# Gate and up of five feed-forward layers made transposed, with the weights held still

## The chip, the core and the metric

The kernel runs on one core of one Trainium2 chip. The metric is the device time in microseconds of one execution, the median over runs. Engines are named as the profile names them: PE is the matrix engine (PEld its weight loads), DVE the vector engine, ACT the scalar engine, POOL the general one, SP the one that issues most transfers.

## The reference, cut

256 tokens of width 1024 pass five gated feed-forward layers (hidden width 2816) with a mixer of attention or convolution between them. One layer of the first block, and the form that the other four have:

```python
def rms_norm(x, g):
    y = x * lax.rsqrt(jnp.mean(x * x, axis=-1, keepdims=True) + EPS)
    return y * g

h = rms_norm(x, norm2_g)                                   # first block
x = x + (silu(h @ w_gate) * (h @ w_up)) @ w_down

def swiglu(h, wg, wu, wd):                                 # second block, four times
    return (silu(h @ wg) * (h @ wu)) @ wd
h = rmsnorm(x, g[0])
x = x + 0.5 * rmsnorm(swiglu(h, wg, wu, wd), g[1])
```

## The kernel before

Tokens are two tiles of 128 rows, t = 0 and 1, whose residual stays in `xres`. Every matrix product is done in three parts for accuracy: each operand is split into a high part (float32r, rounded) and a low part (the rest), and high·high, high·low and low·high are added up in PSUM (`mm3`, lines 270 to 272).

Weights come as blocks of 1 MB (128 partitions by 2048 columns) in the fixed order of `PLAN`. `load` brings a block into one of three `raw` buffers on SP's queue; `split` makes of it two pairs of tiles `wh` and `wl`, one ACT copy (line 240) and one DVE subtraction (line 241) of 1024 columns for each. There are 8 buffers of each kind, so four blocks. `take` hands out the next block and issues the splits ahead of it.

The input of a layer is `xT`, the residual transposed, multiplied by the gain and split: a tile of the high part and a tile of the low part, each with 8 pieces of 128 columns for both t (`norm_in`, lines 306 to 312). The factor 1/rms of a token (`rstd`, one value for each row) isn't in it; it is applied to the results.

In `ffn` the pieces of `xT` (128 by 128) are the stationary operand and 512 columns of weights the moving one. So a bank `mm` gets 128 tokens by 512 hidden columns, for gate and for up, t = 0 and 1: four banks for a chunk of 512 columns, five chunks, and a last one of 256. ACT takes the SiLU of gate times `rstd` (line 455) and DVE multiplies it by up times `rstd` (line 456). The product has the tokens on its rows, and the down projection needs the hidden columns there, so `transposes` turns each tile with 128 by 128 transposes on PE (line 414), and ACT and DVE split what comes out (lines 416 and 417). Transposes of a chunk stand behind the gate of the next chunk, those of the last chunk in the down projection.

The down projection takes 11 blocks into four banks. `ends` then calls `finish` (sum of squares, power -0.5 on POOL, a product with the gain `post`, an addition to `xres`, lines 369 to 382) and `norm_in` of the next layer. The first feed-forward has no `post` and adds its banks to `xres` directly (line 361).

A scheduler sets the order on each engine from priorities; the order that is quoted below is what it made.

Of the kernel before, what the change touches and what calls it, by code (L numbers as in the profile page):

```python
# [53 lines left out]

FF_FULL = 5
FF_LAST = 2560


def ffn_blocks(g, u, d, idx):
    out = []
    for c in range(FF_FULL):
        out += proj_blocks(g, idx, c * 512, 512) + proj_blocks(u, idx, c * 512, 512)
    out += proj_blocks((g, u), idx, FF_LAST, 512)
    for k in range(0, 22, 2):
        out.append((d, idx, k, 2, 0, 1024))
    return out
# [107 lines left out]
class K:  # L176
# [121 lines left out]
    def norm_in(self, t, idx):  # L298

        nc = self.nc  # L300
        xh, xl = self.x_halves(t)
        for b in range(2):
            tp = self.tpt()
            for j in range(4):
                k = b * 4 + j
                nc.tensor.transpose(tp[:, j * P : (j + 1) * P], self.xres[t][:, k * P : (k + 1) * P], self.ident)  # L306
            for j in range(4):
                k = b * 4 + j
                c = slice(k * P, (k + 1) * P)
                g = self.cols[:, C_G + idx * 8 + k : C_G + idx * 8 + k + 1]  # L310
                nc.scalar.activation(xh[:, c], tp[:, j * P : (j + 1) * P], AF.Copy, scale=g)  # L311
                nc.vector.scalar_tensor_tensor(  # L312
                    xl[:, c], tp[:, j * P : (j + 1) * P], g, xh[:, c].bitcast(F32), op0=ALU.mult, op1=ALU.subtract)

    def x_halves(self, t):

        if t == 0:
            self.xT = [self.xp.tile([P, 2 * D], F32R, tag=n, name=self.nm(n)) for n in ("xh", "xl")]
        return [a[:, t * D : (t + 1) * D] for a in self.xT]

    def start(self):

        nc = self.nc
        nc.scalar.dma_start(self.cols[:, C_G : C_G + 8], self.cols_in[:, C_G : C_G + 8])
        self.x_halves(0)
        xh, xl = [a[:, :].rearrange("p (t c) -> p t c", t=2) for a in self.xT]
        parts = []
        for p in range(4):
            r = (self.raw if p < 3 else self.gp).tile(
                [P, 2048], F32, tag="raw" if p < 3 else "bias", name=self.nm("first"))  # L330
            for a, n in ((0, 768), (768, 768)) if p < 2 else ((0, 1536),):
                nc.sync.dma_start(r[:, a : a + n], self.first_in[p][:, a : a + n])
            wh = self.hl.tile([P, 1024], F32R, tag="wh", name=self.nm("wh"))
            wl = self.hl.tile([P, 1024], F32R, tag="wl", name=self.nm("wl"))
            for j in range(2):
                k = 2 * p + j
                c, o = slice(k * P, (k + 1) * P), slice(j * 512, (j + 1) * 512)
                g = self.cols[:, C_G + k : C_G + k + 1]
                x = r[:, j * 768 : j * 768 + 256].rearrange("p (t c) -> p t c", t=2)
                u = r[:, j * 768 + 256 : (j + 1) * 768]  # L340
                nc.scalar.activation(wh[:, o], u, AF.Copy)
                nc.scalar.activation(xh[:, :, c], x, AF.Copy, scale=g)  # L342
                nc.vector.tensor_tensor(wl[:, o], u, wh[:, o].bitcast(F32), op=ALU.subtract)
                nc.vector.scalar_tensor_tensor(  # L344
                    xl[:, :, c], x, g, xh[:, :, c].bitcast(F32), op0=ALU.mult, op1=ALU.subtract)
            parts.append((wh, wl))
        self.blk += [[None, parts[:2]], [None, parts[2:]]]
        self.nload = self.nsplit = 2

    def xlhs(self, t):  # L350
        xh, xl = [a[:, t * D : (t + 1) * D] for a in self.xT]
        return lambda k: (xh[:, k * P : (k + 1) * P], xl[:, k * P : (k + 1) * P])

    def finish(self, t, ps, post, half_scale):

        nc = self.nc
        x = self.xres[t]
        if post is None:
            for h in range(2):
                c = slice(h * 512, (h + 1) * 512)  # L360
                nc.vector.tensor_tensor(x[:, c], x[:, c], ps[h], op=ALU.add)
# [40 lines left out]
    def ffn(self, post_row, half_scale, nxt):  # L402
        nc = self.nc
        post = self.row_bcast(post_row, D) if post_row is not None else None
        hT = {}
        pend = None

        def transposes(p):
            c, cw, hs = p
# [11 lines left out]
        for c in range(FF_FULL + 1):  # L421
            cw, nb = (512, 2) if c < FF_FULL else (256, 2)
            pg = [None, None]
            pu = [None, None]
            if c == 0:
                gb = self.take(nb, 2)
                pg[0], pu[0] = self.mmt(cw), self.mmt(cw)
                for i, b in enumerate(gb):
                    self.block_mm(pg[0], b, self.xlhs(0), 0, i == 0, i == nb - 1)
                ub = self.take(nb, 0)  # L430
                for i, b in enumerate(ub):
                    self.block_mm(pu[0], b, self.xlhs(0), 0, i == 0, i == nb - 1)
                pg[1], pu[1] = self.mmt(cw), self.mmt(cw)
                for ps, bs in ((pg[1], gb), (pu[1], ub)):
                    for i, b in enumerate(bs):
                        self.block_mm(ps, b, self.xlhs(1), 0, i == 0, i == nb - 1)
            elif c == FF_FULL:
                both = self.project()
                for t in range(2):
                    pg[t], pu[t] = both[t][:, :cw], both[t][:, cw:]  # L440
                transposes(pend)
            else:
                for pp in (pg, pu):
                    pp[0], pp[1] = self.mmt(cw), self.mmt(cw)
                    for i in range(nb):
                        (b,) = self.take(1)
                        for t in range(2):
                            self.block_mm(pp[t], b, self.xlhs(t), 0, i == 0, i == nb - 1)
                    if pp is pg and pend is not None:
                        transposes(pend)  # L450
            hs = []
            for t in range(2):
                r = self.rstd[t][:, 0:1]
                sg = self.slot()
                nc.scalar.activation(sg[:, :cw], pg[t], AF.Silu, scale=r)  # L455
                nc.vector.scalar_tensor_tensor(sg[:, :cw], pu[t], r, sg[:, :cw], op0=ALU.mult, op1=ALU.mult)  # L456
                hs.append(sg)
            pend = (c, cw, hs)
        ps = [[self.mmt(), self.mmt()] for _ in range(2)]

        def down(t, b, first, last):
# [5 lines left out]
        for i in range(9):  # L467
            (b,) = self.take(1)
            for t in range(2):
                down(t, b, i == 0, False)  # L470
            if i == 0:
                transposes(pend)
# [7 lines left out]
        self.ends(ps, post, half_scale, nxt)  # L480

    def ends(self, ps, post, half_scale, nxt):
        nc = self.nc
        for t in range(2):
            with self.tc.high_priority(offset=HP):
                self.finish(t, ps[t], post, half_scale)
                if nxt is not None:
                    self.norm_in(t, nxt)
                else:
# [690 lines left out]
```

## Time and profile before

| | us |
|---|---|
| median of 3 runs | 1333.37 (1333.33 to 1336.2) |
| the profiled execution | 1331.7 |
| its span, first to last instruction | 1329.5 |
| mean granted PE clock, share of full speed | 0.995 |
| PE busy | 1301.0 (98%) |
| DVE, ACT, POOL busy | 766.3 (58%), 679.9 (51%), 41.0 (3%) |

The time is that of the span and 2.2 us around it. Matmuls are pipelined: a PE row has the time from a matmul's start to its modelled end, and the next one starts before that end. The pace is read from the starts of rows that follow each other, not from the duration of one.

### The profile page before, as it was taken

Reading aid. Unit: us, or ns where it says so; the run is one execution under the profiler, and the core shown is the slowest. Engines: PE = TensorE matmul, PEld = TensorE weight load, DVE = VectorE, ACT = ScalarE, POOL = GpSimd, SP = SyncE. Lnnn points to the kernel's source line nnn. Section 1 sums busy time; section 2 is a strip of 40 time slices with the busy share of each in tenths; the row PEclk is TensorE's granted clock in tenths of the full one; section 3 lists DMA queues with packets and bytes.
Section 4 is the critical chain, followed back from the end, with each engine's and each line's share of the span. In section 5 each row is a group of like instructions: output and inputs, shape, how many; then the busy total and the mean of one; then the engine's idle time right before and its main releaser. Section 6 shows DMA issues by size and latency. Waiting matters only on the chain.

```text
span 1329.5 us, 16379 instructions
## 1 busy us (share of the span) xinstructions
PE 1301.0 (98%) x6382; PEld 1057.5 (80%) x6382; DVE 766.3 (58%) x1167; ACT 679.9 (51%) x1067; POOL 41.0 (3%) x59
## 2 busy tenths in 40 slices
PE   9789999999999999999999999999999999999997
PEld 7567788888888888777888888888888777888886
DVE  6654655545655548896755555655546555755543
ACT  6455554445545436746644444644435855754431
POOL 0310000000000000000000000000000000000000
PEclk9899999999999999999999999999999999999999
DMA  9943555554555545442465554655454453455540
GB/s 353 285 146 116 190 190 188 191 176 173 192 190 188 189 164 192 143 154 99 152 226 180 189 187 159 237 179 187 172 192 172 162 187 113 177 202 190 190 158 32
DMA packets 37502, 238.10 MB, mean 179 GB/s; under 512 B 4272, under 2 KB 7088, under 8 KB 10416
## 3 DMA queue, kind: packets, MB, share of 16 engines
q1 hardware_dynamic: 36064, 234.31, 50.2%
q0 software_dynamic: 640, 2.16, 0.7%
q8 instruction: 50, 0.82, 0.2%
q10 hardware_dynamic: 720, 0.59, 0.1%
q14 instruction: 28, 0.23, 0.0%
HBM read 235.40 MB, written 1.64 MB: 178 GB/s over the span
## 4 chain that ended last, share of the span: by engine, by line
PE 89%; DVE 3%; ACT 2%; DMA 1%; issue 1%; POOL 0%; ACTq 0%; DVEq 0%; POOLq 0%; SPq 0%
PE mm L272 27%; PE mm L270 27%; PE mm L271 27%; PE tp L414 2%; PE at L621 1%; PE mm L812 1%; PE tp L575 1%; PE tp L306 1%; DVE wl L241 1%; DMA cw<-cw 1%; PE at L690 1%; PE tp L648 1%; PE at L966 0%; ACT e L628 0%; ACT wh L240 0%
## 5 line engine op out<-in xcount | busy, mean ns | idle before, releaser
L241 DVE TENSOR_TENSOR wl<-raw,wh 128x1024 fp32r<-128x1024 f32 (+1 forms) x422 | 508.8, 1219 | 422.4 <-ACT wh L240 409.6
L240 ACT ACTIVATE wh<-raw 128x1024 fp32r<-128x1024 f32 (+1 forms) x422 | 439.5, 1056 | 511.3 <-PE mm L272 474.4
L270 PE MATMUL mm<-wh,xh 128*128 128x512 f32 (+1 forms) x1168 | 459.5, 393 | 1.4 <-ACT xh L342 0.9
L272 PE MATMUL mm<-wh,xl 128*128 128x512 f32 (+1 forms) x1168 | 456.9, 392 | 0.1
L271 PE MATMUL mm<-wl,xh 128*128 128x512 f32 (+1 forms) x1168 | 455.8, 390 | 0.0
L270 PEld LDWEIGHTS mm<-wh,xh 128*128 128x128 f32 x1168 | 220.0, 188 | 47.6 <-ACT xh L311 1.7
L272 PEld LDWEIGHTS mm<-wh,xl 128*128 128x128 f32 x1168 | 219.7, 188 | 46.3 <-DVE xl L344 0.8
L271 PEld LDWEIGHTS mm<-wl,xh 128*128 128x128 f32 x1168 | 220.0, 188 | 44.7 <-issue 0.7
L270 PE MATMUL mm<-wh,slot 128*128 128x512 f32 x536 | 210.5, 393 | 1.3 <-ACT slot L564 1.3
L272 PE MATMUL mm<-wh,slot 128*128 128x512 f32 x536 | 209.5, 391 | 0.6 <-DVE slot L565 0.6
L271 PE MATMUL mm<-wl,slot 128*128 128x512 f32 x536 | 209.5, 391 | 0.0
L270 PEld LDWEIGHTS mm<-wh,slot 128*128 128x128 f32 x536 | 100.7, 188 | 23.3 <-issue 1.7
L272 PEld LDWEIGHTS mm<-wh,slot 128*128 128x128 f32 x536 | 100.7, 188 | 21.8 <-DVE slot L565 1.0
L271 PEld LDWEIGHTS mm<-wl,slot 128*128 128x128 f32 x536 | 100.7, 188 | 19.9
L456 DVE SCALAR_TENSOR_TENSOR slot<-mm,rstd,slot 128x512 f32<-128x512 f32 (+1 forms) x60 | 41.8, 703 | 18.2 <-PE mm L272 18.2
L311 ACT ACTIVATE xh<-tp,cols 128x128 fp32r<-128x128 f32 x112 | 37.3, 370 | 24.8 <-PE tp L306 14.4
L312 DVE SCALAR_TENSOR_TENSOR xl<-tp,cols,xh 128x128 fp32r<-128x128 f32 x112 | 35.6, 347 | 15.4 <-ACT xh L311 14.1
L628 ACT ACTIVATE e<-e,mx 128x128 f32<-128x128 f32 (+1 forms) x80 | 35.3, 445 | 6.9 <-DVE mx L625 6.9
L455 ACT ACTIVATE slot<-mm,rstd 128x512 f32<-128x512 f32 (+1 forms) x60 | 36.4, 657 | 3.5 <-PE mm L272 3.4
L417 DVE TENSOR_TENSOR slot<-tp,slot 128x512 fp32r<-128x512 f32 (+1 forms) x60 | 35.9, 639 | 0.0
L369 ACT ACTIVATE junk<-mm 128x512 bf16<-128x512 f32 x24 | 14.4, 601 | 36.3 <-PE mm L272 36.3
L283 POOL TENSOR_TENSOR pr<-pm,mhalf 128x1 f32<-128x1 f32 x12 | 6.6, 550 | 855.8 <-DVE pm L373 855.8
(122 smaller groups left out, 642.1 us busy)
## 6 DMA issues: line engine op xcount, KB each, us to landing
raw<-w SPq DMA_DIRECT2D x209, 1024.0 KB, 4.9
gb<-rows SPq DMA_DIRECT2D x7, 512.0 KB, 5.5
cw<-cw SPq DMA_DIRECT2D x2, 1024.0 KB, 14.0
bias<-rev SPq DMA_DIRECT2D x2, 1024.0 KB, 5.7
xc<-h POOLq DMA_DIRECT2D x4, 394.5 KB, 13.6
first<-first SPq DMA_DIRECT2D x4, 384.0 KB, 4.5
first<-first SPq DMA_DIRECT2D x2, 768.0 KB, 7.8
raw<-w SPq DMA_DIRECT2D x2, 592.0 KB, 3.7
```

Of the source, the lines that this page charges most:

```text
L240: self.nc.scalar.activation(wh[:, o], r[:, i_], AF.Copy)
L241: self.nc.vector.tensor_tensor(wl[:, o], r[:, i_], wh[:, o].bitcast(F32), op=ALU.subtract)
L270: mm(ps, xh, wh, start=start, stop=False)
L271: mm(ps, xh, wl, start=False, stop=False)
L272: mm(ps, xl, wh, start=False, stop=stop)
L311: nc.scalar.activation(xh[:, c], tp[:, j * P : (j + 1) * P], AF.Copy, scale=g)
L312: nc.vector.scalar_tensor_tensor(xl[:, c], tp[:, j * P : (j + 1) * P], g, xh[:, c].bitcast(F32), op0=ALU.mult, op1=ALU.subtract)
L414: nc.tensor.transpose(tp[:, j * P : (j + 1) * P], hs[t][:, j * P : (j + 1) * P], self.ident)
L417: nc.vector.tensor_tensor(hlo[:, :cw], tp, hh[:, :cw].bitcast(F32), op=ALU.subtract)
L455: nc.scalar.activation(sg[:, :cw], pg[t], AF.Silu, scale=r)
L456: nc.vector.scalar_tensor_tensor(sg[:, :cw], pu[t], r, sg[:, :cw], op0=ALU.mult, op1=ALU.mult)
L628: nc.scalar.activation(s[:, :nk], s[:, :nk], AF.Exp, bias=mx[:, h : h + 1], scale=-1.0, accum_out=sm[:, h : h + 1])
```

## The change

The first 512 columns of gate and up stay as they were. The other 2304 are made in nine pairs of 256 gate and 256 up columns. Now 128 columns of weights are the stationary operand, and the moving one is x: `xT` becomes one tile in which, for each of the 8 pieces, the high part of all 256 tokens and the low part stand side by side (512 columns). `wh` against all 512 columns gives high·high in the left half of a bank and high·low in the right half; `wl` against the left 256 columns adds low·high to the left half. A bank so holds 128 hidden columns by 256 tokens twice, and the two halves are added when it is emptied (an ACT copy, a DVE addition). The result has the hidden columns on its rows, as the down projection needs them; it isn't transposed.

`rstd` now differs along the columns. For gate it is made into a tile `R` by two transposes for each layer (`rstd_rows`) and multiplied in by DVE before the SiLU. For up it is left out: it is one factor of each token, so `finish` applies it to the result of down. The blocks are as many and as large as before.

```diff
+        def cols_T():
+            (b,) = self.take(1)
+            z = self.slot()
+            for f in range(2):
+                bank = self.mmt()
+                for k in range(8):
+                    self.mm3_T(bank, k, *self.part(b, k * 256 + f * P, P), k == 0, k == 7)
+                zf = z[:, f * 256 : (f + 1) * 256]
+                nc.scalar.activation(zf, bank[:, :256], AF.Copy)
+                nc.vector.tensor_tensor(zf, zf, bank[:, 256:], op=ALU.add)
+            return z
+
+        for c in range(FF_PAIRS):
+            g = cols_T()
             if c == 0:
...
+                R = self.rstd_rows()
+            v2 = lambda z: z[:, :].rearrange("p (f n) -> p f n", f=2)
+            nc.vector.tensor_tensor(v2(g), v2(g), R[:, :256].unsqueeze(1).broadcast_to([P, 2, 256]), op=ALU.mult)
+            nc.scalar.activation(g, g, AF.Silu)
+            if c == 0:
+                transposes(pend)
+            u = cols_T()
+            nc.vector.tensor_tensor(g, u, g, op=ALU.mult)
+            hh, hlo = self.slot(F32R), self.slot(F32R)
+            nc.scalar.activation(hh, g, AF.Copy)
+            nc.vector.tensor_tensor(hlo, g, hh[:, :].bitcast(F32), op=ALU.subtract)
+            for f in range(2):
                 for t in range(2):
...
+    def mm3_T(self, bank, k, wh, wl, start, stop):
+
+        x = self.xT[:, k * 512 : (k + 1) * 512]
+        mm = self.nc.tensor.matmul
+        mm(bank, wh, x, start=start, stop=False)
+        mm(bank[:, :256], wl, x[:, :256], start=False, stop=stop)
...
+    def rstd_rows(self):
+
+        nc = self.nc
+        rb, R = self.slot(), self.slot()
+        for t in range(2):
+            nc.vector.tensor_copy(rb[:, t * P : (t + 1) * P], self.rstd[t][:, 0:1].broadcast_to([P, P]))
+        nc.scalar.activation(R[:, :256], self.transpose4(rb, 2), AF.Copy)
+        return R
...
+        if row is not None:
+            r2 = self.small(1, "pr2")
+            nc.vector.tensor_scalar(r2, row, row[:, 0:1], c0, op0=ALU.mult, op1=ALU.mult)
+            c0 = r2[:, 0:1]
...
-                nc.vector.tensor_tensor(y, ps[h], post[:, h * 512 : (h + 1) * 512], op=ALU.mult)
+            pc = post[:, h * 512 : (h + 1) * 512]
+            if row is None:
+                nc.vector.tensor_tensor(y, ps[h], pc, op=ALU.mult)
+            else:
+                nc.vector.scalar_tensor_tensor(y, ps[h], row[:, 0:1], pc, op0=ALU.mult, op1=ALU.mult)
```

On PE, in the first feed-forward of the kernel before, the gate and up of a chunk and the eight transposes behind them stand so (`xh` and `xl` are the two tiles of `xT`):

```order
L270 MATMUL mm_1433<-wh_1448,xh_1233 128x512
L271 MATMUL mm_1433<-wl_1449,xh_1233 128x512
L272 MATMUL mm_1433<-wh_1448,xl_1234 128x512
L414 MATMUL tp_1520<-sh,slot_1426 128x128 x4
L414 MATMUL tp_1529<-sh,slot_1429 128x128 x4
L270 MATMUL mm_1538<-wh_1454,xh_1233 128x512
```

The changed kernel has at that place, where the gate of the first pair ends and its up begins:

```order
L358 MATMUL mm_1478<-xT_1232,wh_1436 128x512
L359 MATMUL mm_1478<-xT_1232,wl_1437 128x256
L612 MATMUL tp_1501<-sh,slot_1497 128x128 x2
L432 MATMUL tp_1507<-sh,slot_1424 128x128 x4
L358 MATMUL mm_1536<-xT_1232,wh_1440 128x512
L359 MATMUL mm_1536<-xT_1232,wl_1441 128x256
```

Three matmuls of 512 columns became one of 512 and one of 256; the two transposes of `rstd` came in (L612), and the transposes of a chunk (now L432) stand only here, four of them and, five matmuls on, four more.

On DVE, in the same layer of the kernel before, the splits (`wl`) of later blocks stand between the products (L456) of a chunk:

```order
L241 TENSOR_TENSOR wl_1619<-raw_1540,wh_1618 128x1024
L241 TENSOR_TENSOR wl_1623<-raw_1540,wh_1622 128x1024
L456 SCALAR_TENSOR_TENSOR slot_1608<-mm_1538,rstd_1294,slot_1608 128x512
L241 TENSOR_TENSOR wl_1653<-raw_1574,wh_1652 128x1024
L456 SCALAR_TENSOR_TENSOR slot_1611<-mm_1539,rstd_1301,slot_1611 128x512
```

The changed kernel has the additions of the bank halves (L468), the product with `R` (L476), the product with up (L481) and the low part of the result (L484) around them, here from the second pair:

```order
L468 TENSOR_TENSOR slot_1589<-slot_1589,mm_1590 128x256
L241 TENSOR_TENSOR wl_1687<-raw_1579,wh_1686 128x1024
L241 TENSOR_TENSOR wl_1691<-raw_1579,wh_1690 128x1024
L468 TENSOR_TENSOR slot_1589<-slot_1589,mm_1609 128x256
L476 TENSOR_TENSOR slot_1589<-slot_1589,slot_1498 128x512
L468 TENSOR_TENSOR slot_1640<-slot_1640,mm_1641 128x256
L241 TENSOR_TENSOR wl_1738<-raw_1630,wh_1737 128x1024
L241 TENSOR_TENSOR wl_1742<-raw_1630,wh_1741 128x1024
L468 TENSOR_TENSOR slot_1640<-slot_1640,mm_1660 128x256
L481 TENSOR_TENSOR slot_1589<-slot_1640,slot_1589 128x512
L484 TENSOR_TENSOR slot_1681<-slot_1589,slot_1680 128x512
```

The addition that empties a block's second bank (`mm_1609`) moved behind the two splits of the block that will use the same `wh` and `wl` buffers four blocks later.

## Rows read from the trace of the kernel before

**Rows 1.** The page: busy time, share of the span, instructions of each engine.

```profile
PE 1301.0 (98%) x6382; PEld 1057.5 (80%) x6382; DVE 766.3 (58%) x1167; ACT 679.9 (51%) x1067; POOL 41.0 (3%) x59
```

**Rows 2.** The page: the chain that ended last, its shares by line.

```profile
PE mm L272 27%; PE mm L270 27%; PE mm L271 27%; PE tp L414 2%; PE at L621 1%; PE mm L812 1%; PE tp L575 1%; PE tp L306 1%; DVE wl L241 1%; DMA cw<-cw 1%; PE at L690 1%; PE tp L648 1%; PE at L966 0%; ACT e L628 0%; ACT wh L240 0%
```

**Rows 3.** Groups by form, PE: busy us, mean ns, idle before.

```profile
L414 PE MATMUL tp<-sh,slot 128*128 128x128 f32 x220 | 28.9, 272 | 0.0
L306 PE MATMUL tp<-sh,xres 128*128 128x128 f32 x112 | 16.5, 277 | 1.6 <-DVE xres L382 1.6
```

**Rows 4.** Timeline of PE, first feed-forward, around transposes: start, duration, group.

```profile
168.33 0.40 PE L272 MATMUL mm<-wh,xl 128*128 128x512 f32 x1
168.56 1.04 PE L414 MATMUL tp<-sh,slot 128*128 128x128 f32 x8
...
169.68 0.40 PE L271 MATMUL mm<-wl,xh 128*128 128x512 f32 x1
169.91 0.39 PE L272 MATMUL mm<-wh,xl 128*128 128x512 f32 x1
...
190.99 0.39 PE L272 MATMUL mm<-wh,xl 128*128 128x512 f32 x1
```

**Rows 5.** Timeline of PE, matmuls of 296 columns in a mixer.

```profile
523.64 0.29 PE L270 MATMUL mm<-wh,xh 128*128 128x296 f32 x1
...
524.32 0.30 PE L272 MATMUL mm<-wh,xl 128*128 128x296 f32 x1
...
526.78 0.30 PE L272 MATMUL mm<-wh,xl 128*128 128x296 f32 x1
```

**Rows 6.** Timeline of PEld, a weight load there.

```profile
524.32 0.19 PEld L270 LDWEIGHTS mm<-wh,xh 128*128 128x128 f32 x1
```

**Rows 7.** Timeline of PE and of PEld, float32 products of 128 columns.

```profile
571.27 0.60 PE L660 MATMUL at<-slot,slot 128*128 128x128 f32 x4
571.71 0.60 PE L575 MATMUL tp<-sh,slot 128*128 128x128 f32 x4
...
572.04 0.53 PEld L660 LDWEIGHTS at<-slot,slot 128*128 128x128 f32 x4
```

**Rows 8.** Groups by form, PEld: busy us, mean ns, idle before.

```profile
L271 PEld LDWEIGHTS mm<-wl,xh 128*128 128x128 f32 x1168 | 220.0, 188 | 44.7 <-issue 0.7 <-DVE wl L343 0.3
L660 PEld LDWEIGHTS at<-slot,slot 128*128 128x128 f32 x24 | 3.0, 191 | 0.4 <-issue 0.3
```

**Rows 9.** Groups by form, DVE and ACT.

```profile
L241 DVE TENSOR_TENSOR wl<-raw,wh 128x1024 fp32r<-128x1024 f32 x418 | 505.7, 1223 | 422.4 <-ACT wh L240 409.6
L240 ACT ACTIVATE wh<-raw 128x1024 fp32r<-128x1024 f32 x418 | 436.9, 1060 | 511.3 <-PE mm L272 474.4 <-issue 15.6 <-DMA raw<-w 12.4
L382 DVE SCALAR_TENSOR_TENSOR xres<-slot,pr,xres 128x512 f32<-128x512 f32 x24 | 17.0, 749 | 1.4
L598 ACT ACTIVATE slot<-tp 128x256 f32<-128x256 f32 x40 | 13.0, 378 | 16.3 <-PE tp L575 16.1
L590 DVE TENSOR_TENSOR slot<-slot,slot 128x512 f32<-128x512 f32 x12 | 8.2, 686 | 0.0
L564 ACT ACTIVATE slot<-slot 128x512 fp32r<-128x512 f32 x10 | 6.3, 633 | 10.6 <-DVE slot L694 10.4
L588 DVE TENSOR_TENSOR slot<-mm,slot 128x256 f32<-128x256 f32 x12 | 5.0, 416 | 0.0
```

**Rows 10.** Timeline of DVE and POOL, the end of the kernel.

```profile
1323.59 0.16 DVE L373 SCALAR_TENSOR_TENSOR pm<-ps,pm 128x1 f32<-128x1 f32 x1 [1.97 <-ACT junk L369]
1323.66 0.68 DVE L378 TENSOR_TENSOR slot<-mm,gb 128x512 f32<-128x512 f32 x1
...
1323.89 0.55 POOL L283 TENSOR_TENSOR pr<-pm,mhalf 128x1 f32<-128x1 f32 x1 [4.89 <-DVE pm L373]
```

More of the change, by code (lines that the diff above doesn't have):

```diff
@@ L53, in proj_blocks @@
     return out
-FF_FULL = 5
-FF_LAST = 2560
+FF_FIRST = 512
+FF_PAIRS = (FF - FF_FIRST) // 256
 def ffn_blocks(g, u, d, idx):
[L62 to L65, printed above, removed]
+    out = proj_blocks(g, idx, 0, FF_FIRST) + proj_blocks(u, idx, 0, FF_FIRST)
+    for c in range(FF_PAIRS):
+        for n in (g, u):
+            out += proj_blocks(n, idx, FF_FIRST + c * 256, 256)
     for k in range(0, 22, 2):
@@ L325, in start @@
         self.x_halves(0)
-        xh, xl = [a[:, :].rearrange("p (t c) -> p t c", t=2) for a in self.xT]
         parts = []
@@ L350, in xlhs, with finish @@
     def xlhs(self, t):
-        xh, xl = [a[:, t * D : (t + 1) * D] for a in self.xT]
-        return lambda k: (xh[:, k * P : (k + 1) * P], xl[:, k * P : (k + 1) * P])
-    def finish(self, t, ps, post, half_scale):
+        xT = self.xT
+        return lambda k: tuple(xT[:, k * 512 + a : k * 512 + a + P] for a in (t * P, 256 + t * P))
+    def mm3_T(self, bank, k, wh, wl, start, stop):
[3 more added lines that the diff above has]
+        mm(bank[:, :256], wl, x[:, :256], start=False, stop=stop)
+    def finish(self, t, ps, post, half_scale, row=None):
         nc = self.nc
@@ L360, in finish @@
                 c = slice(h * 512, (h + 1) * 512)
-                nc.vector.tensor_tensor(x[:, c], x[:, c], ps[h], op=ALU.add)
+                if row is None:
+                    nc.vector.tensor_tensor(x[:, c], x[:, c], ps[h], op=ALU.add)
+                else:
+                    nc.vector.scalar_tensor_tensor(x[:, c], ps[h], row[:, 0:1], x[:, c], op0=ALU.mult, op1=ALU.add)
             return
@@ L377, in finish @@
             y = self.slot()
-            nc.vector.tensor_tensor(y, ps[h], post[:, h * 512 : (h + 1) * 512], op=ALU.mult)
+            pc = post[:, h * 512 : (h + 1) * 512]
+            if row is None:
+                nc.vector.tensor_tensor(y, ps[h], pc, op=ALU.mult)
+            else:
+                nc.vector.scalar_tensor_tensor(y, ps[h], row[:, 0:1], pc, op0=ALU.mult, op1=ALU.mult)
             z.append(y)
@@ L405, in ffn @@
         hT = {}
-        pend = None
+        rs = list(self.rstd)
         def transposes(p):
@@ L419, in transposes @@
                     hT[(t, c * 4 + j)] = (hh[:, j * P : (j + 1) * P], hlo[:, j * P : (j + 1) * P])
[L421 to L424, printed above, removed]
-            if c == 0:
[L426 to L438, printed above, removed]
-                for t in range(2):
[L440 to L458, printed above, removed]
@@ new lines, in ffn @@
+        gb = self.take(2, 2)
+        pg, pu = [self.mmt(), None], [self.mmt(), None]
+        for i, b in enumerate(gb):
+            self.block_mm(pg[0], b, self.xlhs(0), 0, i == 0, i == 1)
+        ub = self.take(2, 0)
+        for i, b in enumerate(ub):
+            self.block_mm(pu[0], b, self.xlhs(0), 0, i == 0, i == 1)
+        pg[1], pu[1] = self.mmt(), self.mmt()
+        for ps, bs in ((pg[1], gb), (pu[1], ub)):
+            for i, b in enumerate(bs):
+                self.block_mm(ps, b, self.xlhs(1), 0, i == 0, i == 1)
@@ new lines, in ffn @@
+        hs = []
+        for t in range(2):
+            sg = self.slot()
+            nc.scalar.activation(sg, pg[t], AF.Silu, scale=self.rstd[t][:, 0:1])
+            nc.vector.tensor_tensor(sg, pu[t], sg, op=ALU.mult)
+            hs.append(sg)
+        pend = (0, 512, hs)
+        def cols_T():
[9 more added lines that the diff above has]
+            return z
@@ new lines, in ffn @@
+        for c in range(FF_PAIRS):
+            g = cols_T()
+            if c == 0:
+                R = self.rstd_rows()
[10 more added lines that the diff above has]
+            for f in range(2):
+                for t in range(2):
+                    o = slice(f * 256 + t * P, f * 256 + (t + 1) * P)
+                    hT[(t, 4 + 2 * c + f)] = (hh[:, o], hlo[:, o])
@@ L470, in ffn @@
                 down(t, b, i == 0, False)
-            if i == 0:
-                transposes(pend)
         bs = self.take(2, 2)
@@ L479, in ffn, with ends @@
                         self.mm3(ps[t][h], *hT[(t, k0 + k)], *self.part(b, k * 1024 + h * 512, 512), False, bi == 1 and k == nk - 1)
-        self.ends(ps, post, half_scale, nxt)
-    def ends(self, ps, post, half_scale, nxt):
+        self.ends(ps, post, half_scale, nxt, rs)
+    def rstd_rows(self):
+        nc = self.nc
+        rb, R = self.slot(), self.slot()
+        for t in range(2):
+            nc.vector.tensor_copy(rb[:, t * P : (t + 1) * P], self.rstd[t][:, 0:1].broadcast_to([P, P]))
+        nc.scalar.activation(R[:, :256], self.transpose4(rb, 2), AF.Copy)
+        return R
+    def ends(self, ps, post, half_scale, nxt, rs=(None, None)):
         nc = self.nc
@@ L485, in ends @@
             with self.tc.high_priority(offset=HP):
-                self.finish(t, ps[t], post, half_scale)
+                self.finish(t, ps[t], post, half_scale, rs[t])
                 if nxt is not None:
```

19 lines of the change are left out of this document (10 added, 9 removed).

## The prediction

> **What bounds the kernel now.** The page's first part comes first: PE is busy for 1301.0 of 1329.5 us, DVE for 58%, ACT for 51% [rows 1]. A busy PE need not be a full one, so the chain that ended last is read next: three lines of one helper, the three matmuls of a split product, hold 27% of the span each, and the transposes of the feed-forward (L414) 2% [rows 2]. Then the idle time by group: before the 220 transposes L414 PE never waits, and before the transposes of the next layer's input (L306) 1.6 us in all [rows 3]. So in the feed-forward layers nothing but PE's own work sets the time, and the change is worth what it takes from or adds to PE's queue, as long as DVE and ACT keep up.
>
> The pace of that queue is read from starts. From 169.91 to 190.99 us stand 93 steps of matmuls of 512 columns, so one takes 21.08 / 93 = 0.2267 us [rows 4], though a row shows 0.39. Among the matmuls of 296 columns 23 steps lie between 523.64 and 526.78, 0.1365 us each [rows 5]. Both have one weight load of 128 columns for each matmul. The slope is (226.7 - 136.5) / 216 = 0.418 ns a column, the remainder 12.9 ns a matmul.
>
> **What is taken from PE.** In each of the five layers 9/11 of the gate and up matmuls change: before, 3 parts x 8 pieces x 2 token tiles x 9 chunk halves = 432 matmuls of 512 columns, 432 x 0.2267 = 97.9 us. After, 9 pairs x 2 x 2 banks x 8 pieces = 288 of 512 and 288 of 256 columns. The columns streamed are as many (221,184); there are 144 more matmuls, each with a load.
>
> The transposes: from the matmul ahead of eight of them (168.33) to the second one behind (169.68) pass 1.35 us, of which two matmuls would take 0.45. So eight cost 0.90 us, 0.112 each [rows 4]. A layer has 44, or 4.93 us; after, 8 of them and the 2 that make `R` stay, 1.12 us. That takes away **3.81 us a layer**.
>
> **What a matmul of 256 columns costs** decides the rest, and the trace has none of this kind. The line through the two paces gives 136.5 - 40 x 0.418 = 119.8 ns. It can't simply be drawn out, because the next weights must be there: a load row lasts 188 ns [rows 8], longer than such a matmul streams. The rows show how far that is hidden. Where a matmul of 296 columns starts (524.32), the load for the next one starts too [rows 5, 6], and yet the pace is 136.5, under the load's 188: most of a load's row is a delay that the next load overlaps. The shortest pace with full loads is that of the float32 products of 128 columns: four loads of 191 ns on average last 0.53 us in all, so (0.53 - 0.19) / 3 = 0.113 us each, and four matmuls take 571.71 - 571.27 = 0.44 us, 0.110 each [rows 7, 8]. Loads can thus follow each other at 110 ns, which is still under 119.8. The bounds: from below 110 (the product of 128 columns as it is; a gain on the line is not excluded), from above 136.5 (the 296 columns, if that is already the pace of a load and not of the columns). I take 119.8, since the loads' own pace stays under it, and because both points share the same remainder.
>
> Then the matmuls of a layer take 288 x (0.2267 + 0.1198) = 99.8 us, **1.86 us more**. Together a layer gains 3.81 - 1.86 = 1.95 us, five layers 9.75 us.
>
> The Trainium skill (TensorE: Matmul & The Clock Gate, Part 3, "The mechanism") says that a weight load runs beside a matmul in flight only if it aims at another group of rows. All loads here fill all rows, so by that rule each of the 144 added loads would be paid. The rows disagree: the load starts with the preceding matmul, and the pace lies under the load's duration [rows 5, 6, 8]. It stands as a rival below.
>
> **What is added on ACT and DVE, and what hides it.** For each pair DVE has four splits (1.223 us), four additions of 256 columns (0.416, the row of L588 that also reads a bank) and three operations of 512 columns (0.686, L590): 4.89 + 1.66 + 2.06 = 8.6 us. ACT has four splits (1.060), four copies of 256 columns (0.378, L598), the SiLU and the high part (0.633 each, L564): 7.0 us [rows 9]. PE needs 32 x 0.3465 = 11.1 us for a pair. Both fit, DVE at 78%.
>
> Order matters more than the sum. The second addition of a block is queued on DVE behind two splits whose `wh` must wait until PE has read the buffers that they overwrite; such waits for PE are the 474.4 us ahead of the ACT splits now [rows 9]. The last of the four parts comes free when that second bank ends; then ACT needs 1.06 us, DVE 1.22, the addition 0.42: the bank is free 2.7 us after its end. With four banks it is wanted two banks later, 2 x 8 x 0.3465 = 5.5 us. So 2.8 us are to spare, and what lies behind it (product with `R`, SiLU, product with up, high and low part) is wanted only in the down projection. The splits stay four blocks ahead. `R` needs two copies on DVE and then its transposes; these stand behind the two banks of the first gate, 5.5 us after `rstd` was needed anyway for the first SiLU. I cost these waits at nothing; without the cover each microsecond by which a bank is late would be paid in every block, 90 times.
>
> **The ends of the layers.** In `finish` the product with `post` goes from 0.68 us (L378) to 0.75 (the form of L382) [rows 9, 10]. At the end of the kernel, where nothing hides it, it ends at 1324.34 now, while POOL's power, needed by the same next step, ends at 1323.89 + 0.55 = 1324.44 [rows 10]. So 0.07 us more stay under it. The one-column factor `r2` falls into the 1.97 us that DVE waits there. The first layer has no POOL in that chain and pays some 0.1 us.
>
> **Sum.** -9.75 + 0.1 = -9.65 us on the profiled execution: 1331.7 - 9.6 = 1322.1. The median of the runs shown lies 1.7 above that execution, so I forecast 1333.4 - 9.6 = **1323.8**. With p the pace in ns of a matmul of 256 columns, the change in us is 5 x 0.288 p - 182.1; it is zero at p = 126.4.
>
> **The rivals.**
>
> *The fixed part is smaller.* With p = 110, as in rows 7, it is 1.44 x 110 - 182.1 = -23.7 us, 1309.7. For it: those rows. Against it: they are float32, not float32r, and the two paces of the same kind agree on a remainder of 12.9 ns. The Trainium skill (the same page, "Wait — 56ns, not 53.3ns?") puts the fixed part of a matmul at about 2.5 ns; the rows here have 12.9. With 2.5 the 144 added matmuls would cost an estimated 0.4 us a layer in place of 1.86, and the time would be 1316.
>
> *The load isn't hidden behind the shorter matmul: slower.* The loads of the next `wh` have only a matmul of 256 columns beside them. If 136.5 is the least pace of a float32r load, the change is +14.5 us, 1348; if the whole 188 ns of the row are paid, +88.6 us, 1422. It decides from 126.4 ns on. For it: no float32r matmul shorter than 296 columns is in the trace, so its loads were never seen faster than 136.5. Against it: the float32 loads of the same size and duration at 110 to 113 [rows 7, 8].
>
> *DVE sets the pace: slower.* If ACT and DVE wait for each other in the new chain, the second addition comes late and PE waits at a bank. From 2.8 us of delay on this is paid; a quarter of a microsecond for each of 90 blocks is 22.5 us, so 1324 + 22 = 1346. For it: DVE goes from under 60% to 78% and stands in strict order behind waits. Against it: the 2.8 us to spare.
>
> *It does nothing that can be measured.* The transposes' gain and the loss by more matmuls cancel, p between 123.7 and 129.2, or small waits of 0.1 us a block eat it up (90 x 0.1 = 9): 1333.
>
> **How the numbers follow.** The forecast, 1319 to 1329 with p from 117 to 123.7, gets 0.60; the smaller fixed part (1310 to 1319) 0.13; the cancelling 0.10; the load that isn't hidden 0.10; DVE as the bound 0.07. A measurement of this kernel tells some 0.3%, 4 us, from no change: faster 0.73, same 0.10, slower 0.17. The range goes from 1311, near the lower bound of p, to 1342, on the way to the two slow cases, most of whose chance is left out above.
>
> **What would show it.** Right: PE starts in gate and up alternate by 0.227 and 0.120 us; PE never waits at line 358; ten transposes a layer; DVE near 78% in gate and up. Wrong: the step behind the 256 columns is above 0.126; L358 waits for DVE or ACT; PE waits longer than now ahead of L306.

## The result, and the profile after

The changed kernel takes 1325.66 us (median of 4 runs, 1324.17 to 1328.53) where the kernel before takes 1333.82: 8.2 us less, a ratio of 0.9938 with the interval [0.9917, 0.9959]. Forecast were 1324 and a gain of 9.6. The profiled execution takes 1325.67 us, its span is 1323.9.

The page's first part, and its chain by line, against [rows 1, 2]:

```profile
PE 1295.3 (98%) x6932; PEld 1076.6 (81%) x6932; DVE 865.8 (65%) x1400; ACT 739.6 (56%) x1242; POOL 42.4 (3%) x59
...
PE mm L358 25%; PE mm L272 15%; PE mm L270 15%; PE mm L271 15%; PE mm L359 13%; PE at L658 1%; PE tp L612 1%; DVE wl L241 1%; PE mm L849 1%; PE tp L306 1%; DMA cw<-cw 1%; PE at L727 1%; PE tp L685 1%; PE at L1003 0%; ACT wh L240 0%
```

PE has 550 matmuls more and is busy for 5.7 us less; DVE has 100 us more to do, and the chain still runs through PE's matmuls. The transposes of the feed-forward (L414, now L432) are gone from it. The groups by form say whether the new matmuls wait; the last number is the idle time before them:

```profile
L358 PE MATMUL mm<-xT,wh 128*128 128x512 f32 x1440 | 502.7, 393 | 0.0
L359 PE MATMUL mm<-xT,wl 128*128 128x256 f32 x1440 | 403.9, 280 | 0.0
```

They never do. Their pace, in the timeline of PE in the second layer:

```profile
380.17 0.39 PE L358 MATMUL mm<-xT,wh 128*128 128x512 f32 x1
380.40 0.28 PE L359 MATMUL mm<-xT,wl 128*128 128x256 f32 x1
380.52 0.39 PE L358 MATMUL mm<-xT,wh 128*128 128x512 f32 x1
...
381.21 0.39 PE L358 MATMUL mm<-xT,wh 128*128 128x512 f32 x1
```

From a long matmul to its short one pass 0.23 us, from there to the next long one 0.12, and three pairs take 381.21 - 380.17 = 1.04 us, 347 ns a pair; 346.5 were forecast. The first layer is another matter:

```profile
180.27 0.40 PE L358 MATMUL mm<-xT,wh 128*128 128x512 f32 x1
180.51 0.28 PE L359 MATMUL mm<-xT,wl 128*128 128x256 f32 x1
180.63 0.40 PE L358 MATMUL mm<-xT,wh 128*128 128x512 f32 x1
...
181.33 0.40 PE L358 MATMUL mm<-xT,wh 128*128 128x512 f32 x1
```

Here three pairs take 1.06 us, 353 ns each, and so it goes to the layer's end, with no wait shown. I call these two the **short** and the **long pace**. The second layer begins at the long pace too: these are rows of its second bank.

```profile
349.33 0.40 PE L358 MATMUL mm<-xT,wh 128*128 128x512 f32 x1
...
350.39 0.40 PE L358 MATMUL mm<-xT,wh 128*128 128x512 f32 x1
```

Three pairs, 1.06 us. In all five layers the first two banks go so; behind the transposes in the third bank four layers go on at the short pace, the first at the long one. Over the 272 pairs that are left the long pace costs 272 x 0.0065 = 1.8 us a layer. It was not forecast.

### The profile page after: what moved, and what is told of

The parts are those of the page before. It is cut to its first block, busy times and chain, and to the rows that moved or that the text cites. A ratio compares the mean times of both kernels' runs of the same rounds, so it can differ in the third digit from the quotient of the medians.

```text
span 1323.9 us, 17937 instructions
## 1 busy us (share of the span) xinstructions
PE 1295.3 (98%) x6932; PEld 1076.6 (81%) x6932; DVE 865.8 (65%) x1400; ACT 739.6 (56%) x1242; POOL 42.4 (3%) x59
## 4 chain that ended last, share of the span: by engine, by line
PE 91%; DVE 3%; ACT 2%; DMA 2%; issue 1%; POOL 0%; ACTq 0%; SPq 0%; DVEq 0%; POOLq 0%
PE mm L358 25%; PE mm L272 15%; PE mm L270 15%; PE mm L271 15%; PE mm L359 13%; PE at L658 1%; PE tp L612 1%; DVE wl L241 1%; PE mm L849 1%; PE tp L306 1%; DMA cw<-cw 1%; PE at L727 1%; PE tp L685 1%; PE at L1003 0%; ACT wh L240 0%
## 5 line engine op out<-in xcount | busy, mean ns | idle before, releaser
L358 PE MATMUL mm<-xT,wh 128*128 128x512 f32 x1440 | 502.7, 393 | 0.0
L359 PE MATMUL mm<-xT,wl 128*128 128x256 f32 x1440 | 403.9, 280 | 0.0
L358 PEld LDWEIGHTS mm<-xT,wh 128*128 128x128 f32 x1440 | 269.6, 187 | 60.6
L359 PEld LDWEIGHTS mm<-xT,wl 128*128 128x128 f32 x1440 | 272.2, 189 | 0.2
L270 PE MATMUL mm<-wh,xT 128*128 128x512 f32 (+1 forms) x448 | 177.6, 396 | 1.6 <-ACT xT L342 1.0
L272 PE MATMUL mm<-wh,xT 128*128 128x512 f32 (+1 forms) x448 | 176.7, 396 | 0.1
L271 PE MATMUL mm<-wl,xT 128*128 128x512 f32 (+1 forms) x448 | 175.5, 392 | 0.0
L467 ACT ACTIVATE slot<-mm 128x256 f32<-128x256 f32 x180 | 66.6, 370 | 67.6 <-PE mm L359 67.6
L270 PEld LDWEIGHTS mm<-wh,xT 128*128 128x128 f32 x448 | 84.8, 189 | 20.0 <-ACT xT L342 1.6
L272 PEld LDWEIGHTS mm<-wh,xT 128*128 128x128 f32 x448 | 84.5, 189 | 17.9 <-DVE xT L311 0.7
L271 PEld LDWEIGHTS mm<-wl,xT 128*128 128x128 f32 x448 | 84.7, 189 | 17.1 <-issue 0.7
L468 DVE TENSOR_TENSOR slot<-slot,mm 128x256 f32<-128x256 f32 x180 | 74.7, 415 | 1.8 <-ACT slot L467 1.8
```

The source lines that it names most:

```text
L270: mm(ps, xh, wh, start=start, stop=False)
L271: mm(ps, xh, wl, start=False, stop=False)
L272: mm(ps, xl, wh, start=False, stop=stop)
L358: mm(bank, wh, x, start=start, stop=False)
L359: mm(bank[:, :256], wl, x[:, :256], start=False, stop=stop)
L467: nc.scalar.activation(zf, bank[:, :256], AF.Copy)
```

## The experiments

**1. The transposes alone.** The kernel before, with its product split straight from the tile; the transposes are left out, so the down projection multiplies a wrong layout.

```diff
-                tp = self.tpt(cw)
-                for j in range(nk):
-                    nc.tensor.transpose(tp[:, j * P : (j + 1) * P], hs[t][:, j * P : (j + 1) * P], self.ident)
+                tp = hs[t][:, :cw]
```

> The kernel before, in which the feed-forward's product is split straight from its tile and never transposed (44 transposes a layer are left out, so the down projection multiplies the wrong layout; every engine but PE does the same work). If the 220 transposes cost PE 0.112 us each, as the prediction's term has it: 220 x 0.112 = 24.6 us less than before, ratio 0.9815. Rival, that they partly fill time in which PE would stand still: less than half of it, ratio above 0.990.

Measured: 1307.09 us against 1332.31, 25.2 less, ratio 0.9806 [0.9792, 0.9821]. That is 0.115 us for each of the 220; 0.112 was read from the starts in [rows 4]. They filled no gap: the whole of their time was on the path.

**2. The matmuls alone.** The changed kernel with 36 transposes a layer put back.

```diff
+            tp = self.tpt()
+            for j in range(4):
+                nc.tensor.transpose(tp[:, j * P : (j + 1) * P], R[:, (j % 2) * P : (j % 2 + 1) * P], self.ident)
             u = cols_T()
```

> The changed kernel with 36 transposes a layer put back on PE behind each gate (their results are used by nobody). What is left of the change is then its matmuls alone. If the gain is the transposes and the matmuls are a loss: the 180 transposes cost 180 x 0.112 = 20.2 us over the changed kernel, about 1346, and that is 12 us slower than before (ratio 1.009): 9.3 by the forecast's matmul term, the rest by the ones that R needs and the slower first layer. Rival, that the transposed matmuls are themselves faster and the transposes were cheap: no slower than before.

Measured: 1351.17 us, 18.9 over before, ratio 1.014 [1.0123, 1.0157]. The direction is shown: without its savings on transposes the new form loses. Against before it is 7 us more than the 12 that were expected. The timeline of PE has both the transposes and the reason:

```profile
390.31 0.40 PE L358 MATMUL mm<-xT,wh 128*128 128x512 f32 x1
...
390.67 0.60 PE L482 MATMUL tp<-sh,slot 128*128 128x128 f32 x4
...
391.45 0.40 PE L358 MATMUL mm<-xT,wh 128*128 128x512 f32 x1
...
395.34 0.40 PE L358 MATMUL mm<-xT,wh 128*128 128x512 f32 x1
...
396.40 0.40 PE L358 MATMUL mm<-xT,wh 128*128 128x512 f32 x1
```

Two pairs with the four transposes take 391.45 - 390.31 = 1.14 us, less 2 x 0.347 leaves 0.45, as forecast. But further on three pairs take 396.40 - 395.34 = 1.06 us: the matmuls go at the long pace. In every layer they do so from the second of the nine added groups on, 240 of the 288 pairs: 240 x 0.0065 = 1.6 us a layer, 7.8 us in all. The expectation had one slow layer in it, 1.9 us; the rest is most of the 7 us.

**3. How short a matmul can be.** Each matmul of 256 columns as two of 128.

```diff
-        mm(bank[:, :256], wl, x[:, :256], start=False, stop=stop)
+        mm(bank[:, :128], wl, x[:, :128], start=False, stop=False)
+        mm(bank[:, 128:256], wl, x[:, 128:256], start=False, stop=stop)
```

> The changed kernel with each matmul of 256 columns made as two of 128, each with its own load: 1440 matmuls and loads more, the same columns. If loads can follow each other only at 110 ns, the two take 220 ns in place of 117: 1440 x 0.103 = 148 us slower than the changed kernel, about 1474. If only columns and a fixed 12.9 ns count, 2 x 66.4 = 133 ns: 23 us, about 1349. If the whole 188 ns of a load row are paid below some length: 2 x 188, 373 us, about 1699.

Measured: 1483.46 us, 157.8 over the changed kernel; 110 ns for each added matmul and load. The timeline of PE, then that of PEld:

```profile
399.88 0.45 PE L358 MATMUL mm<-xT,wh 128*128 128x512 f32 x1
400.17 0.22 PE L359 MATMUL mm<-xT,wl 128*128 128x128 f32 x1
400.23 0.27 PE L360 MATMUL mm<-xT,wl 128*128 128x128 f32 x1
400.34 0.45 PE L358 MATMUL mm<-xT,wh 128*128 128x512 f32 x1
```

```profile
400.17 0.19 PEld L360 LDWEIGHTS mm<-xT,wl 128*128 128x128 f32 x1
400.28 0.19 PEld L358 LDWEIGHTS mm<-xT,wh 128*128 128x128 f32 x1
400.39 0.19 PEld L359 LDWEIGHTS mm<-xT,wl 128*128 128x128 f32 x1
```

The loads now start 0.11 us apart, though each row lasts 0.19. So 0.11 us is the loads' own pace, for float32r too, and with 128 columns the load is the bound. Of the three cases on record the first holds; that the whole 188 ns of a row are paid is out.

**4. The pace of 256 columns by itself.** The long matmuls of seven pieces as two of 256.

```diff
-        mm(bank, wh, x, start=start, stop=False)
+        for c in (slice(0, 512),) if start else (slice(0, 256), slice(256, 512)):
+            mm(bank[:, c], wh, x[:, c], start=start, stop=False)
```

> The changed kernel with the matmuls of 512 columns made as two of 256 for seven of the eight pieces (1260 more matmuls and loads, the same columns), so that streams of three matmuls of 256 stand there. By 0.418 ns a column and 12.9 ns a matmul, two take 239.6 ns in place of 230: between 9.6 and 12.9 ns for each, 12 to 16 us over the changed kernel, about 1340. If a stream of loads needs more than the 117 ns that one short matmul gives it (136.5, as with 296 columns): 2 x 136.5 - 230 = 43 ns, 54 us, about 1380.

Measured: 1340.84 us, 15.2 over the changed kernel, ratio to before 1.0061 [1.0046, 1.0076]. The timeline of PE, where all matmuls have 256 columns:

```profile
399.86 0.29 PE L360 MATMUL mm<-xT,wl 128*128 128x256 f32 x1
399.99 0.40 PE L359 MATMUL mm<-xT,wh 128*128 128x256 f32 x2
400.22 0.28 PE L360 MATMUL mm<-xT,wl 128*128 128x256 f32 x1
...
402.02 0.28 PE L360 MATMUL mm<-xT,wl 128*128 128x256 f32 x1
```

Eighteen matmuls lie between 399.86 and 402.02, 0.120 us each. The forecast drew 119.8 from the line through 296 and 512 columns.

**5. and 6. DVE loaded.** One product, then three, of 512 columns for each block, which read the second bank.

```diff
+                for _ in range(1 * f):
+                    spare = self.gp.tile([P, D], BF16, tag="junk", name=self.nm("spare"))
+                    nc.vector.tensor_tensor(spare[:, :512], bank, self.sh[:, :512], op=ALU.mult)
```

> The changed kernel with one operation more on DVE for each block: a product of 512 columns that reads the block's second bank (0.69 us, its result is used by nobody), queued ahead of the addition that empties that bank. DVE goes from some 8.4 to 9.8 us of a pair's 11.1, the bank comes free some 3.4 us after its end, wanted at 5.5. If there are 2.8 us to spare as worked out: within 1 us of the changed kernel. Rival, DVE is close to being the bound: a quarter of a microsecond a block or more, over 22 us.

Measured: 1330.0 us, ratio 0.998 [0.997, 0.999] against before. By the ratios that is 4 to 6 us over the changed kernel, so the expectation failed. Yet L358 isn't among what PE waited for in its profile, and the second layer, at the short pace, takes no longer than in the changed kernel. These are its first and its last transposed matmul in the timeline of PE:

```profile
344.53 0.39 PE L358 MATMUL mm<-xT,wh 128*128 128x512 f32 x1
...
445.63 0.28 PE L359 MATMUL mm<-xT,wl 128*128 128x256 f32 x1
```

They start 101.10 us apart; in the changed kernel it is 446.96 - 345.81 = 101.15. The first, third and fifth layers run at the long pace (in the first, three pairs in 181.11 - 180.05 = 1.06 us). At equal pace the added operation is shown to cost nothing; that the whole difference is the pace is likely, but the changed kernel didn't run beside it.

> The same with three such operations for each block: DVE would need 8.4 + 6 x 0.69 = 12.5 us a pair, PE 11.1. Here DVE is the bound by the sum: 1.4 us a pair, 45 pairs, some 60 us over the changed kernel, about 1388. If the time stays below 1340, DVE's sum isn't what counts.

Measured in one run: 1340.66 us, 15 over the changed kernel and not 60. The table of PE's waits, and DVE's busy time in a stretch of the second layer, here and in the changed kernel:

```profile
PE mm L358 <- DVE slot L471: 7.4, 15, 0.5
```

```profile
347.00:446.00 99.00, 97.52 (x554) 84.12 (x553) 91.46 (x140) 54.89 (x84) 0.00 (x0) 1.00 0.50 172
```

```profile
347.00:446.00 99.00, 99.00 (x575) 87.08 (x574) 74.13 (x100) 58.14 (x91) 0.00 (x0) 1.00 0.58 197
```

DVE is at 92% here and at 75% in the changed kernel. PE now does wait for the additions that empty its banks, 15 times, 7.4 us in all: the mechanism of the third rival, at a load that the change doesn't reach. The long pace, into which every layer falls sooner or later, is most of the rest of the 15 us. The sum of durations overstated DVE's need: the rows of following operations overlap (the groups of this stretch add up to 102 us, DVE is busy for 91.5). That splits which stand four blocks ahead are caught up later is likely, not shown.

One such wait, in the second layer, tells when a bank is wanted:

```profile
393.06 0.47 PE L358 MATMUL mm<-xT,wh 128*128 128x512 f32 x1 [0.49 <-DVE slot L471]
```

The addition for which PE waits ended at 392.91 and empties the bank whose last matmul was followed by the next bank's first at 383.93, three banks earlier. With four banks in turn, a bank is wanted three banks after its end, 3 x 8 x 0.3465 = 8.3 us; here it came free after 9.0.

**7. All columns transposed.** The first chunk in the new form too.

```diff
-FF_FIRST = 512
+FF_FIRST = 0
```

> The changed kernel with all 2816 columns of gate and up made transposed (no first chunk in the old form, so no transposes but R's). On PE a layer saves 8 transposes (0.9 us, and 0.3 for the second four) and pays 64 pairs of 0.347 in place of 96 matmuls of 0.227: 22.2 - 21.8 = 0.4. By PE's work alone 0.8 us a layer less, 4 us in all, about 1322. Against it: the moving operand holds both token tiles, so the first matmul of a layer waits for the input of the second tile, which the old form needs only after 48 matmuls (10.9 us); if that wait is some 4 us a layer, 20 us more and 16 slower than the changed kernel, about 1342.

Measured: 1361.06 us, ratio 1.0213 [1.02, 1.0226], 35 over the changed kernel. The timeline of PE at the start of the third layer, and the table of its waits:

```profile
651.15 0.39 PE L272 MATMUL mm<-wh,slot 128*128 128x512 f32 x1
656.21 1.12 PE L306 MATMUL tp<-sh,xres 128*128 128x128 f32 x4 [4.68 <-DVE xT L311]
657.93 1.11 PE L306 MATMUL tp<-sh,xres 128*128 128x128 f32 x4 [0.60 <-DVE xT L311]
658.69 0.77 PE L358 MATMUL mm<-xT,wh 128*128 128x512 f32 x1
...
659.48 0.79 PE L358 MATMUL mm<-xT,wh 128*128 128x512 f32 x1
```

```profile
PE tp L306 <- DVE xT L311: 20.9, 8, 5.0
```

The transposes of the next input have nothing between them that PE could do, since the matmuls of the first token tile alone no longer exist: 20.9 us of waiting, as expected. And behind a gap of 4.68 us the clock is low, by the row of the windows (clock third from the end):

```profile
655.00:661.00 6.00, 4.19 (x15) 3.30 (x16) 5.18 (x16) 4.23 (x11) 1.95 (x2) 0.50 0.82 294
```

0.50 is the lower of its two levels, 1.2 and 2.4 GHz, and the pair takes 0.79 us and not 0.35. The mean granted clock of the whole run falls from 0.995 to 0.984. At half clock for 2 x 0.011 x 1359 = 30 us, that is an estimated 15 us lost, which was not expected. Four of the five layers go at the long pace besides. The 512 columns in the old form are what keeps PE busy there.

**8. One wait fewer, and the long pace again.** `R` is transposed into a bank of the other pool.

```diff
-        nc.scalar.activation(R[:, :256], self.transpose4(rb, 2), AF.Copy)
+        tp = self.att()
+        for j in range(2):
+            nc.tensor.transpose(tp[:, j * P : (j + 1) * P], rb[:, j * P : (j + 1) * P], self.ident)
+        nc.scalar.activation(R[:, :256], tp[:, :256], AF.Copy)
```

> The changed kernel with the two transposes of R written into a bank of the other pool, so that the last four transposes of the first chunk don't wait for ACT to empty one of two banks. In the trace of the changed kernel that stretch costs 0.76 us over a bank's usual time where four transposes cost 0.45: 0.3 us a layer, 1.5 us in all, about 1324. That is under what timing can tell; the trace shows it or not. It also shows again whether the first layer runs at 354 ns a pair and the others at 347, as in the profile of the changed kernel, or whether that was a matter of that execution.

Measured: 1329.5 us (12 runs, 1326.15 to 1332.52), ratio 0.9976 [0.9967, 0.9986]: not faster than the changed kernel. Its interval lies just above the changed kernel's two, [0.9917, 0.9959] and, below, [0.9932, 0.9965]. In its profile the second layer, at the short pace in the changed kernel, has the long one, as the timeline of PE shows:

```profile
399.73 0.40 PE L358 MATMUL mm<-xT,wh 128*128 128x512 f32 x1
...
400.79 0.40 PE L358 MATMUL mm<-xT,wh 128*128 128x512 f32 x1
```

Three pairs, 1.06 us. Four of its five layers go so, by the same reading of their starts. The fourth layer goes at the short pace and takes 952.31 - 851.39 = 100.92 us from its first transposed matmul to its last, 0.23 less than the 101.15 of the changed kernel: that is what the wait for the bank was worth. The chip of experiments 5 to 8 didn't run the changed kernel, so whether the many slow layers come from this edit, which puts all ten transposes in one place, or are common on that chip is not shown.

**9. to 11. What the long pace hangs on.** Run on one chip: every second pair turned; all long matmuls of a bank ahead of its short ones; the changed kernel again. Then, on another chip, the first together with experiment 8. The turn is this:

```diff
-        mm(bank, wh, x, start=start, stop=False)
-        mm(bank[:, :256], wl, x[:, :256], start=False, stop=stop)
+        if k % 2 == 0:
+            mm(bank, wh, x, start=start, stop=False)
+        mm(bank[:, :256], wl, x[:, :256], start=False, stop=False)
+        if k % 2 == 1:
+            mm(bank, wh, x, start=False, stop=stop)
```

and the order long, then short:

```diff
-                for k in range(8):
-                    self.mm3_T(bank, k, *self.part(b, k * 256 + f * P, P), k == 0, k == 7)
+                short = [
+                    self.mm3_T(bank, k, *self.part(b, k * 256 + f * P, P), k == 0, k == 7) for k in range(8)]
+                for mm in short:
+                    mm()
```

> The changed kernel with the order of the two matmuls turned for every second piece (512, 256, 256, 512, 512, 256 and so on), the same matmuls. In the traces so far a layer of the changed form runs in one of two paces from its start to its end: 347 ns a pair (230 and 117) or 354 in a pattern of three pairs (233, 236 and 241 behind 113, 120 and 117); with the long ones made as two of 256 all five layers ran alike. If the slow pace needs a long and a short matmul in strict turn, it goes: all layers at 2.77 us a bank, no layer at 2.83, 2 us a slow layer less than the changed kernel beside it, and a smaller spread of its times. Rival, that it belongs to these operands whatever the order: layers at 2.83 among them as before, the same time as the changed kernel.

> The changed kernel with the eight matmuls of 512 columns of a bank first, then the eight of 256. 8 x 0.227 + 8 x 0.120 = 2.776 us a bank in every layer if matmuls of one length have one pace each (0.2267 before, 0.1203 with the long ones halved) and the slow pace comes from turns; then about 2 us for each slow layer of the changed kernel beside it less. If the fast pace of 117 for a short one behind a long one is lost without anything gained: 2.776 at every layer all the same, since the long one then takes 227 and not 230. Rival: some layers at 2.83 us here too.

> The changed kernel once more, on the chip of the other two. Its times then lie some 1.8 us apart for each layer that runs at 354 ns a pair. In its first profile one layer of five did; if that differs from execution to execution, another number of layers does here and the median moves by up to 5 us with it; if it belongs to the first layer, the profile shows the first layer alone again.

> The two edits together: every second pair turned (512, 256, 256, 512), and R's two transposes in a bank of the other pool. Turned, all five layers ran at 2.79 us a bank; the other bank took 0.2 us from a layer at equal pace. If both hold here, every layer is 0.2 us shorter than with the turn alone, 1 us in all: about 1324, ratio 0.993 against before, with a spread of a microsecond or two that comes from the mixers. Rival: a layer at 2.83 us a bank shows up again.

| | median us (range) | ratio to before |
|---|---|---|
| turned | 1324.92 (1323.74 to 1329.29) | 0.994 [0.9924, 0.9956] |
| long, then short | 1325.9 (1324.89 to 1328.12) | 0.9945 [0.9929, 0.996] |
| changed kernel again | 1327.23 (1323.57 to 1329.02) | 0.9948 [0.9932, 0.9965] |
| turned, other bank | 1325.5 (1323.19 to 1325.89) | 0.994 [0.9926, 0.9953] |

The changed kernel again, timeline of PE in its first and in its fourth layer:

```profile
180.23 0.39 PE L358 MATMUL mm<-xT,wh 128*128 128x512 f32 x1
...
181.27 0.39 PE L358 MATMUL mm<-xT,wh 128*128 128x512 f32 x1
```

```profile
900.12 0.40 PE L358 MATMUL mm<-xT,wh 128*128 128x512 f32 x1
...
901.18 0.40 PE L358 MATMUL mm<-xT,wh 128*128 128x512 f32 x1
```

1.04 and 1.06 us for three pairs: now the first layer has the short pace and the fourth the long one. So it doesn't belong to a layer; it changes between executions of one program. In the turned forms it didn't occur: all five layers of each of the two go at 349 ns a pair (2.79 us a bank of eight). With all long ones first, the timeline is the same from bank to bank:

```profile
400.35 1.11 PE L359 MATMUL mm<-xT,wl 128*128 128x256 f32 x8
401.30 2.00 PE L358 MATMUL mm<-xT,wh 128*128 128x512 f32 x8
403.14 1.11 PE L359 MATMUL mm<-xT,wl 128*128 128x256 f32 x8
```

403.14 - 400.35 = 2.79 us, again in every layer. Strict turns of long and short can go at 347 or 353, other orders at 349. The medians differ by less than their intervals, so no order is shown to be faster. What was expected of the turned order came in part: no layer at 2.83 us a bank, but 2.79 and not 2.77, and times that spread as widely (5.6 us) as the changed kernel's (5.5). With the other bank a turned layer takes 101.18 us from first to last, without it 101.27: 0.1 us less and not 0.2.

## Why the prediction was right

**The bound.** PE alone set the time, and the change was worth what it took from PE's queue. Experiments 1 and 2 show both terms apart: the transposes cost their full time, and without that saving the change is a loss. The new matmuls by themselves are no faster than the old ones.

**The transposes** were priced at 0.112 us each and measured at 0.115. That 1.12 us of them stay in a layer was too little. The first six cost 0.66 (from 351.11 to 352.46, less two pairs), as forecast; the second four are these rows of PE and ACT in the changed kernel:

```profile
352.81 0.40 PE L358 MATMUL mm<-xT,wh 128*128 128x512 f32 x1
353.20 0.66 PE L432 MATMUL tp<-sh,slot 128*128 128x128 f32 x4
353.61 0.36 PE L359 MATMUL mm<-xT,wl 128*128 128x256 f32 x1
353.81 0.40 PE L358 MATMUL mm<-xT,wh 128*128 128x512 f32 x1
...
354.17 0.40 PE L358 MATMUL mm<-xT,wh 128*128 128x512 f32 x1
```

```profile
352.77 0.38 ACT L516 ACTIVATE slot<-tp 128x256 f32<-128x256 f32 x1
```

354.17 - 352.81 less two pairs leaves 0.67 where 0.45 was forecast. They start at 353.20, when ACT has emptied the bank of `R`'s transposes (352.77 + 0.38 = 353.15): that `R` takes one of two banks was overlooked. About 0.2 us a layer, 1 us in all; experiment 8, without that wait, has 0.23 less.

**The matmul of 256 columns**, 119.8 ns by the line, is 0.120 us (experiment 4). That both points share a remainder, as the prediction has it for the line, was no support, since a line through two points always does; experiment 4 is the third point. The load stays hidden because loads can start 0.11 us apart (experiment 3); the margin is 10 ns. The rule that was weighed (the Trainium skill, TensorE: Matmul & The Clock Gate, Part 3, "The mechanism": a load runs beside a matmul only in another group of rows) is not what this trace shows: PEld's loads of all rows start with the preceding matmul here too (in the second layer a matmul at 380.17 us, the load for the next one at 380.18). The fixed part of about 2.5 ns (the Trainium skill, the same page, "Wait — 56ns, not 53.3ns?") doesn't fit either: 0.120 us less 256 columns at 0.418 ns leaves 13 ns.

**DVE and ACT** keep up, and PE never waits for a bank (0.0 us at L358). DVE has 75% in that stretch, 78% were forecast. A bank comes free at most 2.8 us after its end (in the second layer an addition ends at 377.35 + 0.41, 2.79 behind the next bank's first matmul at 374.97); 2.7 were reckoned. But the prediction's 2.8 us to spare were too few: a bank is wanted three banks later and not two (experiment 6), so 8.3 - 2.8 = 5.5 us are to spare. The rival is a real mechanism, shown in experiment 6, at 92%.

**The ends** cost nothing that shows: PE waits 0.7 us for `xres` ahead of L306, against the 1.6 of [rows 3], and the end of the kernel takes as long as before.

**What was not in the sum** is the pace of the pairs, 1.8 us in the one layer of the profile, and chance in the mixers. In that profile PE's clock was low for a short stretch of the first mixer, by the row of the windows 108 to 112 us (clock third from the end):

```profile
108.00:112.00 4.00, 4.00 (x14) 2.75 (x15) 0.69 (x1) 1.55 (x4) 0.00 (x0) 0.59 0.78 262
```

At a mean of 0.59 that is 0.41 x 4 = 1.6 us that the profile of before, at 1.00 there, didn't pay. 9.65 forecast, less 1 for the bank, 1.8 for the long pace and 1.6 for the clock gives 5.3. The two profiled executions lie 6.0 us apart, their spans 1329.5 - 1323.9 = 5.6; the 0.9 us that PE waits less ahead of L306 cover the difference. The medians lie 8.2 apart here and 1333.87 - 1327.23 = 6.6 on the chip of experiment 9: the closeness of 8.2 to the forecast is in part luck, and the terms that were left out make the gain smaller.

## What to carry to other kernels

Where PE sets the time, count its work in matmuls as well as columns: a rearrangement with as many columns and more matmuls costs the fixed part of each, here 13 ns, and pays only if it takes something else off PE. Price a matmul of a length that the trace doesn't have from the starts of two lengths that it has, and look for the pace at which loads follow each other: with 256 columns, just above that pace, the line held; with 128, below it, the load's 0.11 us was paid. Before the new form is used everywhere, see what PE does while the next operand is being made: the old form may be what it is busy with.

## What the runs showed that was not expected

Long and short matmuls in strict turn have two steady paces, 347 and 353 ns a pair. In the six profiles of strict turns that begin a layer with a chunk in the old form (the changed kernel twice, experiments 2, 5, 6 and 8), all 30 layers go through their first two banks at the long one, and the transposes behind or in them are where a layer passes to the short one or doesn't: eight of the changed kernel's ten layers do, two of five in each of experiments 5 and 6, one of five in experiment 8. Which ones do differs between executions. From there a layer keeps its pace to its end unless something comes between, and then only the turn from short to long was seen: behind the second group of added transposes in experiment 2 (not behind the first), behind a wait for a bank in experiment 6 (in its first layer behind the second wait, not the first). In other orders of the same matmuls, or with nearly all of one length, the two paces weren't seen. What sets them, no run shows.

A bank that two users share for a moment was worth 0.2 us a layer, less than the 1.8 us of the long pace: the edit that shortens the path (experiment 8) had four slow layers in its profile and was no faster.
